# Pads of 32 bytes between tiles: the same matmuls, with operands that begin in other halves of a 64-byte line

## The chip, the core and the metric

The kernel runs on one core of one Trainium2 chip. The metric is the device time of one execution in microseconds; lower is better. A core has a matrix engine (TensorE, PE in the profile, with its weight loads shown apart as PEld), VectorE (DVE), ScalarE (ACT), GpSimd (POOL) and SyncE (SP), which issues most transfers. SBUF, the on-chip memory, has 128 partitions; a tile takes the same bytes of every partition, so one byte address says where it begins. In this text the *half* of a tile or operand is its first byte's address modulo 64, which is 0 or 32 for everything here.

## The reference: what is computed

One layer of an encoder, with the same weights, over 1024 and 256 tokens, 1024 wide; then a final RMSNorm. All in float32.

```python
n = _rms_norm(h, g_mix, NORM_EPS)
z = jnp.einsum('bsd,dc->bsc', n, w_in)                 # one input projection for both mixers
oa = _diff_attention(q, k, v, lam, slopes)             # 4 heads, two softmax maps each
ob = _gqa_attention(qb, kb, vb)                        # 8 query heads, 2 kv heads, rotary positions
h = h + jnp.einsum('bsc,cd->bsd', mixed, w_out)
n2 = _rms_norm(h, g_mlp, NORM_EPS)
a = jax.nn.relu(jnp.einsum('bsd,df->bsf', n2, w_ff1))  # 1024 -> 4096
h = h + jnp.einsum('bsf,fd->bsd', a * a, w_ff2)        # 4096 -> 1024
gate = jax.nn.sigmoid(jnp.einsum('bsd,de->bse', _rms_norm(h, g_ple, NORM_EPS), w_ple_gate))
h = h + gate * jnp.einsum('bsp,pd->bsd', p_l, w_ple_proj)
```

## The kernel before

**Products.** A float32 product is made of three matmuls of type float32r. Each operand is split into a high part (ScalarE copies it, rounded, into a float32r tile) and a low part (VectorE or GpSimd subtracts the high part from the original). The matmuls are high·high, high·low and low·high, accumulated in one PSUM bank. A matmul has a *stationary* operand of 128 columns, which a weight load brings into the array, and a *moving* operand of 128, 256, 384 or 512 columns, which streams through it. In the profile's names `out<-a,b` on PE, `a` is the moving operand and `b` the stationary one. The weight load of the next matmul runs while the present one streams, so what is read from SBUF at the same time is the moving operand of one matmul and the stationary operand of the next.

**Stages**, with their place in the profiled span. The order of the instructions on each engine is fixed in the program.

1. Input projections, to about 260 us: `psb` and `psv` take the weights as moving operand (256 columns) and the tokens `xh`, `xl` as stationary; `psa` the other way round, with 512 or 256 columns.
2. Attention with the output projection woven in, to about 750 us. `sc` are the scores, `tr` transposes of the probabilities, `av` the products with the values (`plan_unit.av`, line 720: moving `ph`, `pl`, 256 columns; stationary the value tile `vt128` or `vt256`). `pso` is the output projection (moving weights `ow`, 512 columns; stationary `mt`).
3. First MLP product, to about 1200 us, by Strassen's scheme: seven products for each of 16 column blocks of `w_ff1`. `Unit1.put` runs one product for two pieces of the tokens, 384 and 256 columns. Each piece is a run of 12 matmuls into one PSUM tile: eight with the moving operand `nhi` (the high part of the tokens, slots H0 to H6), then four with `nlo` (the low part, slots L1 to L7). Stationary is `w1` in a W slot. That is 7 × 16 = 112 runs of each length.
4. Second MLP product, to about 1547 us, again seven products, each over eight blocks (`NB`), so m = 0 to 55. `put2` runs 30 matmuls of 512 columns for each m: five tiles j of six matmuls. Moving is `wo`, stationary `ao`. The slots rotate with m % 3 (line 1339): `ao` in H0, H2, H3, and `wo` in H1, L7, L5.
5. Gate and embedding, to the end: ten token tiles; for each, eight transposes (`trg`), then twice 24 matmuls `psg` (moving the gate weights `gw`, stationary `n3`, 512 columns) followed by six matmuls `psp` (moving `pw`, stationary `p_h`, `p_l`). The last tile is cut into more pieces of 512 and 256 columns. `gate` has the elementwise work behind each `psg`, and lines 1601 to 1632 that of the embedding and the final norm.

**Where tiles begin.** Tiles come from pools that are stacked in SBUF from the left and from the right. A pool of `slot`s holds one buffer for each tag, and later tiles of other shapes take the same slot. `open_out_proj` opens the slots H0 to H6 and W0 to W8 on the right; L1 to L7, Q, K and W9 to W11 lie on the left. `TILES` lists the attention's buffers in the order in which they are laid down. The addresses below are read from the two built programs.

Of the kernel before, what the change touches and what calls it, by code (L numbers as in the profile page):

```python
# [14 lines left out]
F32 = mybir.dt.float32  # L15
F32R = mybir.dt.float32r
F16 = mybir.dt.float16
# [6 lines left out]
P = 128  # L24
D = 1024
KD = D // P
NP_TOK = 1024
NS_TOK = 256
T = NP_TOK + NS_TOK
NT = T // P  # L30
# [4 lines left out]
DISTW = 1920  # L35
# [5 lines left out]
def f(ap):  # L41
    return ap.bitcast(F32)
# [3 lines left out]
def encoder_kernel(ctx: ExitStack, tc: tile.TileContext, x, xT, pT, w_in, w_out, w_ff1, w_ff2, w_gate, w_proj,  # L46
# [11 lines left out]
    PHB = 4  # L58
# [37 lines left out]
    def pool(name, bufs=1, side=None, space=None, stack=None):  # L96
        kw = dict(name=name, bufs=bufs, reuse_waits="tile")
        if side:
            kw["side"] = side
        if space:  # L100
            kw["space"] = space
        return (stack or ctx).enter_context(tc.tile_pool(**kw))
# [32 lines left out]
    def rsqrt(dst, src, scale, eps, tp, n, tag):  # L135
        vv = tp.tile([P, n], F32, tag=f"{tag}v", name=f"{tag}v")
        uu = tp.tile([P, n], F32, tag=f"{tag}u", name=f"{tag}u")
        V.tensor_scalar(vv, src, scale, eps, op0=ALU.mult, op1=ALU.add)
        S.activation(uu, vv, AF.Ln)
        S.activation(dst, uu, AF.Exp, scale=-0.5)  # L140
        if n == 1:
            S.activation(uu, dst, AF.Copy, scale=-0.5)
            V.scalar_tensor_tensor(vv, dst, dst, vv, op0=ALU.mult, op1=ALU.mult)
            V.scalar_tensor_tensor(dst, vv, -3.0, uu, op0=ALU.add, op1=ALU.mult)
            return
        V.tensor_tensor(uu, dst, dst, op=ALU.mult)
        V.tensor_tensor(uu, uu, vv, op=ALU.mult)
        V.tensor_scalar(uu, uu, -0.5, 1.5, op0=ALU.mult, op1=ALU.add)
        V.tensor_tensor(dst, dst, uu, op=ALU.mult)
# [45 lines left out]

    def slot(tag, shape, dt, name):
        return slot_pool[tag].tile(shape, dt, tag=tag, name=name, bufs=1)

    def open_slots(pool_, tags):
        for tag in tags:  # L200
            slot_pool[tag] = pool_
            size = {"H": 2560, "L": 2560, "W": 1024, "Q": 1280, "K": 1280, "T": 512}[tag[0]]
            slot(tag, [P, size], F32, tag)
# [264 lines left out]
    def early_w1():  # L468
        for p in range(NEW):
            raws = [slot(f"Q{kh}", [P, 4, 256], F32, "w1e") for kh in range(2)]  # L470
            for kh, raw in enumerate(raws):
                load(raw, w_ff1[kh * 512:kh * 512 + 512, p * 256:(p + 1) * 256].rearrange("(k p) c -> p k c", p=P))
# [28 lines left out]
    def along(main, side, skip, every):  # L501
# [20 lines left out]
    TILES = {  # L522
        "o": ([P, 256], F32, 3), "or": ([P, 256], F32, 1), "ml": ([P, 2, 256], F32R, 1),
        "mm": ([P, 2], F32, 4), "ll": ([P, 2], F32, 4), "rl": ([P, 2], F32, 4), "osq": ([P, 256], F32, 1),
        "kt": ([P, T], F32R, 1), f"vt{P}": ([P, NT, P], F32R, 1), "ph": ([P, 2, 256], F32R, PHB),
        "pl": ([P, 2, 256], F32R, PLB), "qt": ([P, 2, 2, 256], F32R, QTB), "p": ([P, 1024], F32, PB),
        "dist": ([P, DISTW], F16, 1), f"vt{2 * P}": ([P, NT, 2 * P], F32R, 1), "pq": ([P, 256], F32, 4),
    }

    MT = 0  # L530
# [314 lines left out]
    def open_out_proj():  # L845
        xs.close()
        fr = pool("fr", side="right")
        open_slots(fr, [f"H{i}" for i in range(7)] + [f"W{i}" for i in range(9)])
        op_state["h"] = [slot(f"H{j}", [P, 2560], F32, "h_sb") for j in range(NT // 2)]

    TORD = (0, 1, 2, 3, 8, 9, 4, 5, 6, 7)
# [22 lines left out]
    def opw_split(raws):  # L874
        n = next(ow_n) % 5
        if n < 2:
            w = slot(f"H{5 + n}", [P, 2, D], F32R, "ow")
            a, b = w[:, 0], w[:, 1]
        else:
            a, b = (slot(f"W{2 * n - 4 + i}", [P, D], F32R, "ow")[:] for i in range(2))  # L880
        for i, raw in enumerate(raws):
            c = slice(i * 512, i * 512 + 512)
            S.activation(a[:, c], raw, AF.Copy)  # L883
            G.tensor_tensor(b[:, c], raw, f(a[:, c]), op=ALU.subtract)
        return a, b
# [504 lines left out]
    def load_h(half, n, tag):  # L1390
        t = hq[half, n] = slot(tag, [P, HP, 512], F32, "hq")
        dma(t, hd[half][:, :, n * 512:n * 512 + 512])
# [6 lines left out]
    def put2(m):  # L1399
        n, b = divmod(m, NB)  # L1400
        ah, al, bh, bl = OPS.pop(m)
        if b == 0:
            if O2[n] in (1, 7):
                acc[O2[n]] = slot({1: "H5", 7: "L4"}[O2[n]], [P, HP, 512], F32, "acc")
            banks_of[n] = [bank(tag, "f2_") for tag in BANKS[n].split()]
        for j in range(HP):
            c = slice(j * P, (j + 1) * P)
            pr = []
            for k in range(2):
                pr += [(ah[:, k, c], bh[:, k]), (ah[:, k, c], bl[:, k]), (al[:, k, c], bh[:, k])]  # L1410
            split3(banks_of[n][j], pr, b == 0, b == NB - 1)
            if b == NB - 1:
                evac2(O2[n], j, banks_of[n][j])
# [52 lines left out]
    gw, pw, n3 = [], [], {}  # L1466
    g_n = itertools.count()

    def w_raw(src):
        n = next(g_n)  # L1470
        t = slot("W10" if n < 4 else f"W{8 + n % 2}", [P, D], F32, "graw")
        dma(t, src)
        return t

    def gate_w(k, tags):
        raw = w_raw(w_gate[k * P:(k + 1) * P, :])
        if len(tags) == 1:
            t = slot(tags[0], [P, 2, D], F32R, "gw")
            a, b = t[:, 0], t[:, 1]
        else:  # L1480
            a, b = (slot(t, [P, D], F32R, "gw")[:] for t in tags)
        S.activation(a, raw, AF.Copy, scale=gple[:, k:k + 1])
        V.scalar_tensor_tensor(b, raw, gple[:, k:k + 1], f(a), op0=ALU.mult, op1=ALU.subtract)
        gw.append((a, b))

    def proj_w(k, tag):
        raw = w_raw(w_proj[k * P:(k + 1) * P, :])
        t = slot(tag, [P, 2, D], F32R, "pw")
        S.activation(t[:, 0], raw, AF.Copy)
        V.tensor_tensor(t[:, 1], raw, f(t[:, 0]), op=ALU.subtract)  # L1490
        pw.append((t[:, 0], t[:, 1]))

    gi_n = itertools.count()

    def h_half(t, n):
        j, half = divmod(TORD.index(t), 2)
        return h_of(j, half, n)

    def gate_input(t):

        n3_ = slot(("H5", "L4")[next(gi_n) % 2], [P, 2, KD, P], F32R, "n3")
        n3h, n3l = n3_[:, 0], n3_[:, 1]
        for n in range(2):
            tr = pp2[0].tile([P, 4, P], F32, tag="tr", name="trg", bufs=2)
            for k in range(4):
                PE.transpose(tr[:, k], h_half(t, n)[:, k * P:(k + 1) * P], ident)
            S.activation(n3h[:, 4 * n:4 * n + 4], tr, AF.Copy)
            V.tensor_tensor(n3l[:, 4 * n:4 * n + 4], tr, f(n3h[:, 4 * n:4 * n + 4]), op=ALU.subtract)
        ss = gq_.tile([P, 2], F32, tag="gss", name="gss")
        for n in range(2):  # L1510
            jk = gq_.tile([P, 512], F32, tag="gjk", name="gjk", bufs=1)
            S.activation(jk, h_half(t, n), AF.Square, accum_out=ss[:, n:n + 1])
        V.tensor_tensor(ss[:, 0:1], ss[:, 0:1], ss[:, 1:2], op=ALU.add)
        rn = gq_.tile([P, 1], F32, tag="grn", name="grn")
        rsqrt(rn, ss[:, 0:1], 1.0 / D, 1e-6, gq_, 1, "grs")
        S.activation(rn, rn, AF.Copy, scale=-1.0)
        return n3h, n3l, rn

    QUADS = {2: (0, 0, "H6"), 3: (0, 1, "L2"), 4: (1, 0, "H4"), 5: (1, 1, "L3")}
    for m in range(NM):  # L1520
        put2(m)
        if m in QUADS:
            load_h(*QUADS[m])
        if m + 3 < NM:
            prep(m + 3)

        if m >= 4 * NB and m % 4 == 0 and len(gw) < 4:
            gate_w(len(gw), KTS[2 * len(gw):2 * len(gw) + 2])
        if m == NM - 4:
            fqs.close()  # L1530
            gq_ = pool("gq", side="left", bufs=2)
            for k in range(2):
                gate_w(4 + k, (ARS[k],))
        elif m == NM - 3:
            gate_w(6, (AOS[m % 3],))
            gate_w(7, (WOS[m % 3],))
            n3[FORD[0]] = gate_input(FORD[0])
        elif m == NM - 2:
            proj_w(0, AOS[m % 3])
            proj_w(1, WOS[m % 3])  # L1540
            n3[FORD[1]] = gate_input(FORD[1])
# [4 lines left out]
    for ti, t in enumerate(FORD):  # L1546
# [70 lines left out]
        i = 2 if last else 1  # L1617
        V.tensor_tensor(ss[:, 0:1], ss[:, 0:1], ss[:, i:i + 1], op=ALU.add)
        if last:

            for (n0, nn), e in zip(pieces[1:], es[1:]):
                V.tensor_tensor(e, h_half(t, 1)[:, n0 - 512:n0 - 512 + nn], gfin[:, n0:n0 + nn], op=ALU.mult)
        rf = gq_.tile([P, 1], F32, tag="rf", name="rf")
        rsqrt(rf, ss[:, 0:1], 1.0 / D, 1e-6, gq_, 1, "rf")
        if last:
            for (n0, nn), e in zip(pieces[1:], es[1:]):
# [2 lines left out]
        for n0 in range(0, 512 if last else D, 512):  # L1629
            n = slice(n0, n0 + 512)  # L1630
# [54 lines left out]
```

## Time and profile before

| | |
|---|---|
| device time, median of 3 runs | 1704.38 us (1703.62 to 1708.34) |
| span of the profiled execution, first to last instruction | 1703.2 us |
| PE busy | 1666.5 us, 98% |
| PEld, DVE, ACT, POOL busy | 87%, 69%, 51%, 39% |
| granted TensorE clock, mean | 0.997 |

No time other than the span is given for the profiled execution itself; the median of the runs is 1.2 us above it. A matmul's duration in the profile reaches past the start of the next one, since matmuls are pipelined: a lone one of the 512-column kind shows some 393 ns, while they start every 227 to 235 ns. So the number that counts is the *pace*, the time from one start to the next. It is read from two views: the chain of waits, whose pieces give the time that a run of matmuls took and their number, and the timeline, whose rows give the start of each run.

### The profile page before, as it was taken

Reading aid. Unit: us, or ns where it says so; the run is one execution under the profiler, and the core shown is the slowest. Engines: PE = TensorE matmul, PEld = TensorE weight load, DVE = VectorE, ACT = ScalarE, POOL = GpSimd, SP = SyncE. Lnnn points to the kernel's source line nnn. Section 1 sums busy time; section 2 is a strip of 40 time slices with the busy share of each in tenths; the row PEclk is TensorE's granted clock in tenths of the full one; section 3 lists DMA queues with packets and bytes.
Section 4 is the critical chain, followed back from the end, with each engine's and each line's share of the span. In section 5 each row is a group of like instructions: output and inputs, shape, how many; then the busy total and the mean of one; then the engine's idle time right before and its main releaser. Section 6 shows DMA issues by size and latency. Waiting matters only on the chain.

```text
span 1703.2 us, 27269 instructions
## 1 busy us (share of the span) xinstructions
PE 1666.5 (98%) x9849; PEld 1488.6 (87%) x9849; DVE 1177.2 (69%) x2119; ACT 868.3 (51%) x1749; POOL 658.4 (39%) x647
## 2 busy tenths in 40 slices
PE   8999999999899999999999999999999999999997
PEld 8999889888788888889999999998888888888886
DVE  7788588787887878578666666665655865445666
ACT  8543377677766767674333233333433333354644
POOL 1224455555653445424655666520533400001441
PEclk9999999999999999999999999999999999999999
DMA  9767844433953624495343434359666466532111
GB/s 316 228 225 246 233 141 124 138 92 108 269 156 118 165 69 127 134 308 181 132 156 127 138 131 150 122 198 376 202 216 195 130 205 193 169 114 73 35 44 50
DMA packets 191867, 278.28 MB, mean 163 GB/s; under 512 B 13674, under 2 KB 121076, under 8 KB 191732
## 3 DMA queue, kind: packets, MB, share of 16 engines
q1 hardware_dynamic: 189988, 271.28, 49.7%
q0 software_dynamic: 1600, 5.24, 1.0%
q8 instruction: 78, 1.28, 0.3%
q14 instruction: 57, 0.47, 0.1%
q10 hardware_dynamic: 144, 0.00, 0.0%
HBM read 182.63 MB, written 88.61 MB: 159 GB/s over the span
## 4 chain that ended last, share of the span: by engine, by line
PE 79%; DVE 7%; ACT 4%; issue 4%; DMA 3%; POOL 3%; SPq 0%; POOLq 0%; ACTq 0%; DVEq 0%
PE psa L255 6%; PE sc L642 5%; PE psb L255 5%; PE av L720 5%; PE pso L255 4%; PE tr L696 3%; PE psv L255 3%; PE psg L1576 2%; DVE pl L707 1%; DMA h_sb<-in_x 1%; DVE mm L659 1%; PE f__16295 L156 1%; PE f__15255 L156 1%; PE f__16637 L156 1%; PE f__15600 L156 1%
## 5 line engine op out<-in xcount | busy, mean ns | idle before, releaser
L1373 ACT ACTIVATE ao<-ar 128x1280 fp32r<-128x1280 f32 x56 | 71.3, 1275 | 187.5 <-PE f__16299 L156 37.8
L642 PE MATMUL sc<-kt,qt 128*128 128x512 f32 (+1 forms) x576 | 157.0, 392 | 6.9 <-ACT p L667 4.6
L707 DVE TENSOR_TENSOR pl<-tr,ph 128x512 fp32r<-128x512 f32 x204 | 137.9, 684 | 33.5 <-ACT ph L702 32.3
L1375 DVE TENSOR_TENSOR ao<-ar,ao 128x1280 fp32r<-128x1280 f32 x56 | 93.3, 1666 | 94.0 <-ACT ao L1373 94.0
L702 ACT ACTIVATE ph<-tr 128x512 fp32r<-128x512 f32 x204 | 119.8, 595 | 56.9 <-PE tr L696 50.4
L255 PE MATMUL pso<-ow,mt 128*128 128x512 f32 x480 | 119.4, 395 | 4.2 <-ACT ow L883 1.8
L696 PE MATMUL tr<-ident,p 128*128 128x128 f32 x768 | 116.0, 274 | 5.7 <-DVE pl L707 4.9
L642 PEld LDWEIGHTS sc<-kt,qt 128*128 128x128 f32 x576 | 99.4, 190 | 24.8 <-ACT p L667 6.1
L1576 PE MATMUL psg<-gw,n 128*128 128x512 f32 (+1 forms) x504 | 115.4, 384 | 0.0
L696 PEld LDWEIGHTS tr<-ident,p 128*128 128x128 f32 x768 | 91.8, 141 | 22.5 <-DVE pl L707 8.6
L1576 PEld LDWEIGHTS psg<-gw,n 128*128 128x128 f32 x504 | 90.8, 188 | 19.5
L255 PEld LDWEIGHTS pso<-ow,mt 128*128 128x128 f32 x480 | 87.5, 188 | 22.4 <-DVE osq L747 2.0
L1094 POOL TENSOR_SCALAR w1r<-w1r,gmlp 128x256 f32<-128x256 f32 x112 | 79.7, 728 | 67.6 <-DMA w1r<-in_w_ff 67.6
L720 PE MATMUL av<-ph,vt 128*128 128x256 f32 x544 | 102.4, 289 | 1.1 <-ACT ph L702 0.5
L681 POOL TENSOR_SCALAR p<-p,rl 128x1024 f32<-128x1024 f32 x64 | 76.0, 1188 | 51.3 <-DVE rl L679 46.6
L1167 ACT ACTIVATE w<-w1s 128x512 fp32r<-128x512 f32 x56 | 35.2, 628 | 116.5 <-POOL w1s L1174 49.4
L659 DVE TENSOR_REDUCE mm<-sc 128x1 f32<-128x1024 f32 (+1 forms) x80 | 84.2, 1055 | 8.8 <-PE sc L642 8.3
L720 PE MATMUL av<-pl,vt 128*128 128x256 f32 x408 | 89.5, 301 | 0.0
L720 PEld LDWEIGHTS av<-ph,vt 128*128 128x128 f32 x544 | 82.4, 190 | 6.6 <-ACT ph L702 0.9
L667 ACT ACTIVATE p<-sc,mm 128x1024 f32<-128x1024 f32 x64 | 71.3, 1114 | 25.5 <-DVE mm L659 18.5
L655 DVE CUSTOM_DVE_ANT_0 p<-sc,dist 128x1024 f32<-128x1024 f32 x64 | 77.6, 1218 | 7.9 <-PE sc L642 3.8
L664 ACT ACTIVATE p<-p,mm 128x1024 f32<-128x1024 f32 x64 | 73.5, 1149 | 18.0 <-DVE mm L655 17.3
(1520 smaller groups left out, 4717.2 us busy)
## 6 DMA issues: line engine op xcount, KB each, us to landing
ar<-ad SPq DMA_DIRECT2D x56, 640.0 KB, 4.0
w2r<-in_w_ff SPq DMA_DIRECT2D x56, 512.0 KB, 4.6
qt<-qd SPq DMA_DIRECT2D x160, 128.0 KB, 3.1
ad<-q SPq DMA_DIRECT2D x64, 320.0 KB, 3.0
ad<-qs SPq DMA_DIRECT2D x48, 320.0 KB, 2.2
w1r<-in_w_ff SPq DMA_DIRECT2D x28, 512.0 KB, 4.3
md<-ml SPq DMA_DIRECT2D x40, 256.0 KB, 2.5
mt<-md SPq DMA_DIRECT2D x20, 512.0 KB, 5.4
```

Source lines behind the costliest of these rows:

```text
L255: PE.matmul(ps, a, b, start=i == 0, stop=i == n - 1)
L642: PE.matmul(ps[:, h0:h0 + n], shared["q"][:, cc, v, i * P:(i + 1) * P], kt[:, s0 + h0:s0 + h0 + n], start=v == 0, stop=v == 1)
L655: V.tensor_tensor_reduce(out=p[:, :sn], in0=ps[:, :sn], in1=dst_t[:, off:off + sn], scale=SLOPES[idx], scalar=3.0e38, op0=ALU.add, op1=ALU ...
L659: V.tensor_reduce(out=st["m", i][:, 0:1], in_=ps[:, :sn], axis=AX.X, op=ALU.max, negate=True)
L681: G.tensor_scalar(p[:, :sn], p[:, :sn], rl[:, 0:1], 1.0, op0=ALU.mult, op1=ALU.mult)
L696: PE.transpose(t[:, jj, i * P:(i + 1) * P], st["ws"][i][:, j * P:(j + 1) * P], ident)
L702: S.activation(ph, st["tr", j2], AF.Copy)
L707: V.tensor_tensor(pl, st["tr", j2], f(st["ph", j2][:]), op=ALU.subtract)
L720: PE.matmul(st["av"][:, :256], x_, y_, start=j2 == 0 and n == 0, stop=j2 == nj - 1 and n == len(pr) - 1)
L1094: G.tensor_scalar(raw[:, k], raw[:, k], gmlp[:, 4 * kh + k:4 * kh + k + 1], 1.0, op0=ALU.mult, op1=ALU.mult)
L1375: V.tensor_tensor(ao[:, 1], a, f(ao[:, 0]), op=ALU.subtract)
L1576: ends[:] = [PE.matmul(ps, a, b, start=m == 0, stop=m == len(pr) - 1)]
```

## The change

The instructions, their order on every engine, their waits and their semaphore updates are the same in both built programs. What differs is where tiles begin, in four ways.

- Small unused tiles of 8 float32 (32 bytes for each partition) are laid down between others: `pad0` to `pad3` ahead of and behind the two value tiles in `TILES`, one between the H and the W slots, and `gpad` at the start of the last stage's pool `gq`.
- `slot32` makes a tile 8 elements longer than asked for and returns the view from the eighth element on, so that it begins 32 bytes into its slot. `at32` is the same function. The output projection's weights in H5 and H6, the single-slot gate weights, the embedding weights `pw` and the normed tokens `n3` use them.
- Ahead of that, the slots H0 to H6 have moved down by 32 bytes through the pad between H and W.
- The tile `rf` has one buffer where it had two, which makes room for `gpad`.

| matmul, columns | count | half of the moving operand: before, after | half of the stationary operand: before, after |
|---|---|---|---|
| `av<-ph,vt` and `av<-pl,vt`, 256 | 952 | 0, 0 | 0, **32** |
| `pso<-ow,mt`, 512 | 480 | 32, 32 | 32, 32 |
| first MLP product, `nhi,w1`, 384 and 256 | 872 of each | 32, **0** | 32, 32 |
| first MLP product, `nlo,w1`, 384 and 256 | 436 of each | 0, 0 | 32, 32 |
| first MLP product with `w1` in W9 to W11 (3 runs of each length): `nhi` | 24 of each | 32, **0** | 0, 0 |
| second MLP product, `wo` in L7 or L5, 512 | 1110 | 0, 0 | 32, **0** |
| second MLP product, `wo` in H1, 512 | 570 | 32, **0** | 32, **0** |
| `psg<-gw,n`, 512 and 256 | 504 | 0 in 189, 32 in 315; after **32** in all | 0 in 264, 32 in 240; after **32** in all |
| `psp<-pw,p`, 512 and 256 | 126 | 32, 32 | 0, **32** |

All other matmuls keep their halves (`psb`, `psv`, `psa`, `sc`), or are transposes whose stationary input moves (`h_sb`, `hq`). Before, every matmul operand with half 0 begins below byte 110,000 of its partition and every one with half 32 above byte 120,000. After, `ao`, `nhi` and the `wo` in H1 begin above 120,000 with half 0, and `vt`, `p_h` and `p_l` below 110,000 with half 32.

```diff
+    def slot32(tag, shape, dt, name):
+        n = int(np.prod(shape[1:]))
+        t = slot(tag, [P, n + 8], dt, name)[:, 8:]
+        dims = " ".join("abc"[:len(shape) - 1])
+        return t.rearrange(f"p ({dims}) -> p {dims}", **dict(zip("abc", shape[1:]))) if len(shape) > 2 else t
+
+    def at32(tag, *args):
+        return slot32(tag, *args)
...
-        "kt": ([P, T], F32R, 1), f"vt{P}": ([P, NT, P], F32R, 1), "ph": ([P, 2, 256], F32R, PHB),
+        "kt": ([P, T], F32R, 1), "pad0": ([P, 8], F32, 1), f"vt{P}": ([P, NT, P], F32R, 1), "pad1": ([P, 8], F32, 1), "ph": ([P, 2, 256], F32R, PHB),
...
-        "dist": ([P, DISTW], F16, 1), f"vt{2 * P}": ([P, NT, 2 * P], F32R, 1), "pq": ([P, 256], F32, 4),
+        "dist": ([P, DISTW], F16, 1), "pad2": ([P, 8], F32, 1), f"vt{2 * P}": ([P, NT, 2 * P], F32R, 1), "pad3": ([P, 8], F32, 1), "pq": ([P, 256], F32, 4),
...
-        open_slots(fr, [f"H{i}" for i in range(7)] + [f"W{i}" for i in range(9)])
+        open_slots(fr, [f"H{i}" for i in range(7)])
+        fr.tile([P, 8], F32, name="pad")
+        open_slots(fr, [f"W{i}" for i in range(9)])
...
-            w = slot(f"H{5 + n}", [P, 2, D], F32R, "ow")
+            w = slot32(f"H{5 + n}", [P, 2, D], F32R, "ow")
...
-            t = slot(tags[0], [P, 2, D], F32R, "gw")
+            t = at32(tags[0], [P, 2, D], F32R, "gw")
...
-        t = slot(tag, [P, 2, D], F32R, "pw")
+        t = at32(tag, [P, 2, D], F32R, "pw")
...
-        n3_ = slot(("H5", "L4")[next(gi_n) % 2], [P, 2, KD, P], F32R, "n3")
+        n3_ = at32(("H5", "L4")[next(gi_n) % 2], [P, 2, KD, P], F32R, "n3")
...
             gq_ = pool("gq", side="left", bufs=2)
+            gq_.tile([P, 8], F32, name="gpad", bufs=1)
...
-        rf = gq_.tile([P, 1], F32, tag="rf", name="rf")
+        rf = gq_.tile([P, 1], F32, tag="rf", name="rf", bufs=1)
```

## The prediction, made before the changed kernel was run

> **What bounds the kernel now.** I read the page's first part and the span first, then the busy time by stretches, then the chain of waits and the timeline inside each stage. The page and the stretches:
>
> ```profile
> span 1703.2 us, 27269 instructions
> PE 1666.5 (98%) x9849; PEld 1488.6 (87%) x9849; DVE 1177.2 (69%) x2119; ACT 868.3 (51%) x1749; POOL 658.4 (39%) x647
> ```
> ```profile
> core 0: us, PE busy (x) PEld busy (x) DVE busy (x) ACT busy (x) POOL busy (x), PEclk, DMA share, GB/s
> 400.00:740.00 340.00, 325.09 (x1963) 280.21 (x1963) 263.91 (x508) 235.51 (x496) 167.29 (x184) 0.99 0.53 155
> 790.00:1190.00 400.00, 400.00 (x2633) 393.82 (x2633) 258.53 (x419) 138.95 (x264) 195.02 (x185) 1.00 0.49 171
> 1240.00:1540.00 300.00, 300.00 (x1303) 243.64 (x1302) 168.79 (x152) 113.53 (x131) 45.23 (x21) 1.00 0.54 173
> 1540.00:1703.20 163.20, 153.74 (x731) 126.72 (x729) 102.53 (x188) 82.02 (x216) 48.79 (x40) 0.98 0.13 45
> ```
>
> In the two MLP stages (790 to 1540 us) PE never stops, at full granted clock, and the busiest other engine, VectorE, has 258.53 of 400 us and 168.79 of 300. There a nanosecond of pace is a nanosecond of the end. In the attention (400 to 740) PE stands 15 of 340 us. So the question is what sets the pace of matmuls that wait for nothing. The chain of waits in the second MLP product shows matmuls of one shape at two paces (pieces of one tile j, six matmuls of 512 columns; columns: start, length, what):
>
> ```profile
> 1302.85 1.39 PE f__15255 L156 x6
> 1305.60 1.36 PE f__15257 L156 x6
> 1308.32 1.36 PE f__15259 L156 x6
> 1309.68 1.40 PE f__15255 L156 x6
> 1322.28 1.40 PE f__15259 L156 x6
> ```
>
> 1.36 / 6 = 226.7 ns, 1.40 / 6 = 233.3 ns. By the slots, the five tiles from 1302.85 have `wo` in H1 (moving half 32, stationary 32: the *same* half), those from 1309.68 on have it in L7, then L5 (0 and 32: *different* halves). The gate stage has all four pairs in one line of code, at 512 columns:
>
> ```profile
> 1549.14 3.40 PE psg L1576 x15
> ```
> ```profile
> 1552.54 1.40 PE psg L1576 x6
> ```
> ```profile
> 1562.92 2.10 PE psg L1576 x9
> ```
> ```profile
> 1565.02 1.39 PE psg L1576 x6
> ```
> ```profile
> 1555.79 1.38 PE psg L1576 x6
> ```
>
> In order: 32 and 32 run 226.7; moving 0 with stationary 32 run 233.3; moving 32 with stationary 0 run 233.3; 0 and 0 run 231.7 in the first six matmuls after a different pair. The last row is 32 and 32, again the first six behind something else: 230. So a same pair needs about six matmuls to settle, and up to there 0 with 0 looks like 32 with 32. That is the reading on which the forecast rests: at 512 columns the *relation* of the two halves sets the pace, 226.7 same and 233.3 different.
>
> With shorter moving operands the relation works the other way round. The first MLP product, chain first (runs of 12), then the timeline (starts; a length there reaches past the next start):
>
> ```profile
> 907.35 1.43 PE f__11906 L156 x12
> 908.78 2.11 PE f__11949 L156 x12
> ```
> ```profile
> 905.08 1.58 PE L156 MATMUL f__11893<-nhi,w 128*128 128x384 f32 x8
> 906.49 0.86 PE L156 MATMUL f__11893<-nlo,w 128*128 128x384 f32 x4
> 907.19 1.12 PE L156 MATMUL f__11906<-nhi,w 128*128 128x256 f32 x8
> 908.15 0.64 PE L156 MATMUL f__11906<-nlo,w 128*128 128x256 f32 x4
> 908.62 0.69 PE L156 MATMUL f__11949<-nhi,w 128*128 128x384 f32 x3
> ```
> ```profile
> 757.99 1.55 PE L156 MATMUL f__10408<-nhi,w 128*128 128x384 f32 x8
> 759.38 0.87 PE L156 MATMUL f__10408<-nlo,w 128*128 128x384 f32 x4
> ```
> ```profile
> 776.91 1.10 PE L156 MATMUL f__10504<-nhi,w 128*128 128x256 f32 x8
> 777.84 0.40 PE L156 MATMUL f__10524<-nlo,w 128*128 128x256 f32 x2
> ```
> ```profile
> 25.18 5.60 PE psv L255 x48
> ```
>
> `nhi` with `w1` in a right-hand slot is a same pair (32, 32): (906.49 − 905.08) / 8 = 176 ns at 384 columns and 0.96 / 8 = 120 at 256. `nlo` is a different pair (0, 32): 0.70 / 4 = 175 and 0.47 / 4 = 117.5. The two rows at 757.99 and 776.91 are the few runs with `w1` on the left, where `nhi` is a different pair: 1.39 / 8 = 173.8 and 0.93 / 8 = 116.3. And `psv`, a different pair (0, 32) in a long run of 256 columns: 5.60 / 48 = 116.7.
>
> **The change part by part.** No instruction and no wait is added, so each part is a count of matmuls by a difference of paces.
>
> *Second MLP product.* 56 blocks m of 5 × 6 matmuls; `wo` lies in L7 or L5 in 37 of them, in H1 in 19. All become 0 and 0. 37 × 5 × (1.40 − 1.36) = 7.4 us. The first piece behind a change of relation (1.39 instead of 1.36) falls away in the 19 others: 19 × 0.03 = 0.6. I take 7.8, the rows being rounded; bounds 8.0, and +0.4 (a loss) if 0 with 0 stayed at the 1.39 that its first six show: 185 × (1.39 − 1.40) + 95 × (1.39 − 1.36) − 0.6.
>
> *First MLP product.* 109 of 112 runs of each length become different pairs throughout. With 173.8 and 116.7 a run takes 2.09 and 1.40: (0.02 + 0.03) × 109 = 5.5, and with 116.3 for all 256-column ones 5.9. With the paces of `nlo`, 175 and 117.5, it is 2.10 and 1.41: 3.3. I take 5.0, nearer to the first, since those rows are eight in a row as the changed ones are. The three runs with `w1` on the left become same pairs and lose under 0.2 us.
>
> *Gate and embedding.* One tile's matmuls, with `n3` on the left:
>
> ```profile
> 1562.23 5.58 PE psg L1576 x24
> 1567.80 1.40 PE psp L156 x6
> 1569.20 5.58 PE psg L1576 x24
> 1574.78 1.40 PE psp L156 x6
> 1577.06 5.57 PE psg L1576 x24
> 1582.65 0.70 ACT ge L1580
> ```
> ```profile
>   ACT ge L1580: 34.1, 18
> ```
>
> That is 13.96 us for 60 matmuls; all same they take 60 × 0.2267 = 13.60 and some 0.04 to settle, 0.32 less. The next tile, with `n3` at 32, begins with 5.57, so it has nearly as much to gain. Nine tiles: 2.9, the upper bound. Against it: from 1582.65 on the chain of waits runs over ScalarE and VectorE, which follow PE closely here. The last row (who waited for `psg`) says that ScalarE still stood waiting for PE, 34.1 us in 18 times, 1.9 on average, before the exponential of each gate half; PE needs to gain 0.16 a half, so most of that cover stays. If it did not, only the two tiles before 1582 gain: 0.6. I take 2.2.
>
> *Attention.* The 952 `av` matmuls go from same (0, 0) to different (0, 32):
>
> ```profile
> 553.73 2.63 PE av L720 x22
> ```
> ```profile
> PE tr L696 <- DVE pl L707: 5.1, 9, 1.1
> PE sc L642 <- ACT p L667: 4.6, 6, 1.7
> ```
>
> 119.5 ns now against 116.7 for a different pair: at most 952 × 2.8 = 2.7 us. They come in fours and sixes between transposes and scores, too short to settle, and PE waits in this stage for VectorE and ScalarE, which get no faster. Between 0 and 2.7 I take 1.0.
>
> *The other engines* write to moved tiles. VectorE's `n3` subtraction, which alternates between half 0 and half 32, shows no difference (smallest, median and largest duration in ns):
>
> ```profile
> L1508 DVE TENSOR_TENSOR n<-trg,n x20: 679/691/692, 1535.3 to 1670.3; 128x512 fp32r<-128x512 f32 x20
> ```
>
> I cost them at nothing. `rf` with one buffer brings no wait, since the two programs' waits are equal.
>
> *Sum.* 7.8 + 5.0 + 2.2 + 1.0 = 16.0 us. On the profiled span that is 1703.2 − 16.0 = 1687.2, and on the median of the runs, 1.2 above the span, 1704.4 − 16.0 = 1688.4. All bounds low: 8.0 + 5.9 + 2.9 + 2.7 = 19.5, so 1684.9. With the second product at 7.4 and the others at 3.3, 0.6 and 0: 11.3, so 1693.1.
>
> **The rivals.**
>
> *It is not the half but the place.* Before the change each half goes with one end of SBUF: 0 below byte 110,000, 32 above 120,000. Every row above would read the same if matmuls met the weight load differently when both operands lie at one end. Pads of 32 bytes then do nothing: 1704.4. For it: no row separates the two. Against it: the sign turns between 512 and 384 columns within differences of 3 to 7 ns, which looks like two streams that fall in or out of step, and a shift of 8 elements is 3 to 4 ns at 226.7 ns for 512.
>
> [...]
>
> *0 with 0 does not settle at 512 columns.* The second product gives its +0.4 and the rest stays: 1704.4 + 0.4 − 5.0 − 2.2 − 1.0 = 1696.6. For it: no row shows 0 with 0 beyond the first matmuls. Against it: row for row these equal 32 with 32.
>
> *The moving operand's half alone decides at 512 (32 fast), and the place in the run, not the half, decides in the shorter ones.* Then H1's blocks fall from 1.36 to 1.40: 19 × (5 × 0.04 − 0.03) = +3.2; the 171 gate matmuls whose moving half goes from 0 to 32 win 171 × 6.6 ns = 1.1; the first product and `av` stay. 1706.5, slower. It decides if the 0 with 0 row keeps 1.39 or more in steady state. Against it: the row 1562.92 has moving 32 and runs 233.3.
>
> **How the numbers follow.** Forecast 0.78 (own range 1685 to 1693), place instead of half 0.11, 0 with 0 unsettled 0.08, moving half alone 0.03. The likeliest time is 1688.4. The forecast and the unsettled case hold 0.86 together, so the range reaches from a little under the lowest bound, 1683, to 1697. About 0.3%, 5 us, is what a measurement can tell from no change. Faster by more: nearly all of the forecast and of the unsettled case, 0.83. Within: the place, and what these two miss, 0.14. Slower: 0.03.
>
> **What would show it.** In the second product every piece of six at 1.36, none at 1.40; if they read 1.39, 0 with 0 does not settle. In the first product runs of 12 at 2.08 to 2.10 and 1.40 to 1.41, still with no idle PE. In the gate 24 matmuls in 5.45 to 5.50, and ScalarE's wait before L1580 smaller but there. Pieces at 1.36 and 1.40 alternating as before would show that the place decides. I am wrong, too, if the paces come as forecast and the end does not: then VectorE or ScalarE bounds the last stage.

## The result, and the profile after

The changed kernel takes 1690.83 us (median of 4 runs, 1689.4 to 1692.11) against 1704.76 before: a ratio of 0.9915, with a 95% interval of 0.9902 to 0.9927. A second set of five runs gave 1692.16, ratio 0.9921 (0.9908 to 0.9935). The forecast was 1688.4 with a range of 1683 to 1697. The profiled execution took 13.1 us less than before, the forecast's sum is 16.0. What follows is mostly about those 3 us, and about what the word "half" in the forecast stands for.

The page of the changed kernel, its first part:

```profile
span 1690.1 us, 27269 instructions
PE 1651.6 (98%) x9849; PEld 1482.7 (88%) x9849; DVE 1179.9 (70%) x2119; ACT 868.0 (51%) x1749; POOL 661.0 (39%) x647
```

The busy time by stretches, with the columns as in the prediction (the two MLP stages, then the last stage):

```profile
785.00:1185.00 400.00, 400.00 (x2666) 394.32 (x2665) 261.51 (x424) 139.45 (x265) 199.84 (x191) 1.00 0.50 174
1235.00:1533.00 298.00, 298.00 (x1324) 246.63 (x1323) 173.30 (x155) 114.84 (x134) 44.26 (x21) 1.00 0.54 175
1533.00:1690.10 157.10, 146.08 (x704) 122.34 (x702) 97.95 (x185) 79.28 (x212) 48.77 (x40) 0.98 0.12 43
```

PE still never stops in the MLP stages, at the same granted clock, but 2666 matmuls begin in 400 us where 2633 did. The changed kernel's line numbers are higher by 9 in the attention and by 12 in the gate: L1588 is `psg` (L1576 before), L1592 the exponential `ge` behind it (L1580 before).

The second MLP product, in the chain of waits (start, length, what):

```profile
1290.99 1.36 PE f__15262 L156 x6
...
1296.43 1.36 PE f__15261 L156 x6
...
1310.04 1.36 PE f__15261 L156 x6
```

Of 222 whole pieces of six that the chain shows between 1228 and 1534 us, 219 read 1.36, whichever slot `wo` has; none alternates with 1.40. The first product, in the chain and then in PE's timeline:

```profile
898.35 1.42 PE f__11837 L156 x12
899.76 2.09 PE f__11862 L156 x12
```
```profile
898.19 1.11 PE L156 MATMUL f__11837<-nhi,w 128*128 128x256 f32 x8
899.13 0.63 PE L156 MATMUL f__11837<-nlo,w 128*128 128x256 f32 x4
899.60 1.56 PE L156 MATMUL f__11862<-nhi,w 128*128 128x384 f32 x8
901.00 0.86 PE L156 MATMUL f__11862<-nlo,w 128*128 128x384 f32 x4
901.69 1.11 PE L156 MATMUL f__11875<-nhi,w 128*128 128x256 f32 x8
```

At 384 columns `nhi` takes 1.40 / 8 = 175 and `nlo` 0.69 / 4 = 172.5 ns. At 256 columns it is 0.94 / 8 = 117.5 and 0.47 / 4 = 117.5, in a run of 1.42 us where 1.40 to 1.41 was forecast. The gate, in the chain, and who waited for `psg`:

```profile
1549.62 5.50 PE psg L1588 x24
1555.13 1.36 PE psp L156 x6
1556.49 5.44 PE psg L1588 x24
1561.93 1.38 PE psp L156 x6
...
1563.34 0.93 POOL hq L1615
```
```profile
  ACT ge L1592: 25.2, 14
```

24 matmuls take 5.50 and 5.44 us where they took 5.58, so PE does what was forecast. ScalarE's wait for it went from 34.1 us in 18 times to 25.2 in 14. The attention, where 22 `av` matmuls took 2.63:

```profile
553.65 2.60 PE av L729 x22
```

Where the time went, by the starts in both timelines (a pace is the mean of the start-to-start times that hold no wait; the change in us is over all starts of the group):

| part | pace before, after (ns) | change, us | forecast |
|---|---|---|---|
| second MLP product, 512 columns | 231.4, 226.7 | −7.6 | −7.8 |
| first product: `nhi` 384; `nhi` 256 | 177.2, 174.4; 119.5, 118.4 | −3.5 | |
| first product: `nlo` 384; `nlo` 256 | 174.3, 173.4; 118.7, 118.0 | −0.8 | −5.0 with the row above |
| gate and embedding, `psg` at 512 | 231.7, 227.6 | −2.3 with `psp` | −2.2 |
| attention: `ph`; `pl` | 119.1, 118.0; 118.8, 117.2 | −1.5 with its waits (−1.25 by the paces alone) | −1.0 |
| all other starts, waits among them | | +1.1 | 0 |
| from the last matmul's start to the end | | **+1.5** (9.74, now 11.27) | 0 |

With 0.1 less ahead of the first matmul that makes the 13.1. `nlo` and `w1` keep their halves, and still `nlo` became faster by 0.7 to 0.9 ns; it runs right behind `nhi`, which moved, and it is back at its old paces when `nhi` alone goes back (w1_undone, below). So the pace of a pair is not fixed by its two starts alone. The waits of the attention vary from run to run: over the profiles of the kernels whose value tiles lie as in the change, the `av` groups, waits included, differ from before by −2.5 to +0.2 us.

The row of +1.5 us is the one that the forecast did not have. ScalarE's exponentials of the last tiles in its timeline, and PE's last groups, of the kernel before:

```profile
1678.32 0.69 ACT L1580 ACTIVATE ge<-psg,grn 128x512 f32<-128x512 f32 x1 [0.96 <-PE psg L1576]
1686.80 0.67 ACT L1580 ACTIVATE ge<-psg,grn 128x512 f32<-128x512 f32 x1
```
```profile
1679.52 11.42 PE L1576 MATMUL psg<-gw,n 128*128 128x512 f32 x72
```

and of the changed kernel:

```profile
1664.12 0.67 ACT L1592 ACTIVATE ge<-psg,grn 128x512 f32<-128x512 f32 x1
1673.64 0.67 ACT L1592 ACTIVATE ge<-psg,grn 128x512 f32<-128x512 f32 x1
```
```profile
1658.11 5.60 PE L1588 MATMUL psg<-gw,n 128*128 128x512 f32 x24
1664.91 11.36 PE L1588 MATMUL psg<-gw,n 128*128 128x512 f32 x72
```

Before, ScalarE waited 0.96 us for PE at 1678.32, and then took the last tile's first piece 7.28 us after its matmuls began. Now it waits for PE neither time (no bracket), and takes that piece 8.73 us after its matmuls began, 1.45 us later. The matmuls have moved ahead of the elementwise work of the tile before, and the time that they gained waits there.

### The profile page after: what moved, and what is told of

Same layout as the page of the kernel before. It is cut to its first block, busy times and chain, and to the rows that moved or that the text cites. A ratio compares the mean times of both kernels' runs of the same rounds, so it can differ in the third digit from the quotient of the medians.

```text
span 1690.1 us, 27269 instructions
## 1 busy us (share of the span) xinstructions
PE 1651.6 (98%) x9849; PEld 1482.7 (88%) x9849; DVE 1179.9 (70%) x2119; ACT 868.0 (51%) x1749; POOL 661.0 (39%) x647
## 4 chain that ended last, share of the span: by engine, by line
PE 79%; DVE 8%; ACT 4%; issue 4%; POOL 2%; DMA 2%; POOLq 0%; SPq 0%; ACTq 0%; DVEq 0%
PE psa L264 6%; PE sc L651 6%; PE av L729 5%; PE psb L264 4%; PE pso L264 4%; PE tr L705 4%; PE psv L264 2%; PE psg L1588 1%; DVE pl L716 1%; DVE p L686 1%; DMA xt<-in_x 1%; POOL hq L1615 1%; DMA xr<-in_xT 1%; PE f__15605 L156 1%; PE f__16642 L156 1%
## 5 line engine op out<-in xcount | busy, mean ns | idle before, releaser
L1588 PE MATMUL psg<-gw,n 128*128 128x512 f32 (+1 forms) x504 | 113.7, 381 | 0.0
L1588 PEld LDWEIGHTS psg<-gw,n 128*128 128x128 f32 x504 | 90.9, 188 | 17.8
```

The source lines that it names most:

```text
L1588: ends[:] = [PE.matmul(ps, a, b, start=m == 0, stop=m == len(pr) - 1)]
```

## The experiments

All were run with the changed kernel as their base unless it is said otherwise. They fall into three groups: is it the relation of the two starts, and part by part; what is the relation's period; and what takes the 1.5 us at the end. `slot_at(off, ...)` is `slot32` with `off` elements of 4 bytes in the place of 8.

### The second product alone made different: w2_diff

```diff
-        wo = slot(WOS[m % 3], [P, 2, 2, 512], F32R, "wo")
+        wo = slot_at(8, WOS[m % 3], [P, 2, 2, 512], F32R, "wo")
```

> The changed kernel, with the moving operand wo of the second MLP product 32 bytes into its slots (32) against ao at 0, so that all 1680 matmuls of that stage are different pairs. Theory (the relation of the two halves sets the pace, 226.7 ns same and 233.3 ns different at 512 columns): every piece of six takes 1.40 us, the stage 1680 x 6.6 ns = 11.1 us more, about 1702 us. Rival (the moving operand's own half decides, 32 is fast): pieces stay at 1.36 us, about 1691 us.

Measured: 1701.78 us, ratio to the kernel before 0.9983 (0.9974 to 0.9992). Pieces in the chain:

```profile
1325.13 1.40 PE f__15609 L156 x6
1326.54 1.40 PE f__15605 L156 x6
```

All of the second product has the slow pace, 233.3 ns on average, also the blocks that were at 1.36 in the kernel before. 1701.8 − 1690.8 is 11.0 us (9.6 from the change's second set); 1680 × (233.3 − 226.7) ns is 11.1. The moving operand now has the half 32 throughout, so the rival that a moving half of 32 is fast by itself at 512 columns falls. That it is a matter of the place in SBUF falls too: `wo` and `ao` lie in the slots where they lay.

### The first product alone put back: w1_undone

```diff
         open_slots(fr, [f"H{i}" for i in range(7)])
-        fr.tile([P, 8], F32, name="pad")
         open_slots(fr, [f"W{i}" for i in range(9)])
...
-            w = slot32(f"H{5 + n}", [P, 2, D], F32R, "ow")
+            w = slot(f"H{5 + n}", [P, 2, D], F32R, "ow")
...
     def at32(tag, *args):
-        return slot32(tag, *args)
+        return (slot if tag[0] == "H" else slot32)(tag, *args)
...
-        wo = slot(WOS[m % 3], [P, 2, 2, 512], F32R, "wo")
+        wo = slot_at(0 if WOS[m % 3][0] == "H" else 8, WOS[m % 3], [P, 2, 2, 512], F32R, "wo")
```

Without the pad the H slots begin 32 bytes higher; the tiles in them that began 32 bytes into their slot begin at its start now, which is the same address. The second product has 32 with 32, and the first has what it had before the change.

> The changed kernel without the pad between the H and W slots, so that nhi is at 32 again as w1 is (same pairs, as before the change); wo in L5 and L7 is put at 32 so that the second product keeps same pairs (32 and 32), and gate, embedding and attention keep their halves. Theory: the first product's runs of 12 go back to 2.11 and 1.43 us, which is worth the 4 to 5 us that they gained; 1695 to 1696 us; the second product stays at 1.36 for six, with wo in the low end of SBUF and ao in the high one. Rival (the place in SBUF sets the pace and 32 bytes do nothing): no stage moves, 1691 us, or the second product shows 1.40 wherever wo and ao lie at different ends.

Measured: 1694.98 us, ratio 0.9946 (0.9929 to 0.9962), 4.2 us more than the change (2.8 more than its second set). The first product's runs of 12 in the chain:

```profile
898.36 1.43 PE f__11836 L156 x12
899.79 2.11 PE f__11861 L156 x12
```

These are the lengths before the change, and the four mean paces are back to 177.1, 174.3, 119.5 and 118.7. The second product stays at 226.8 with both operands at 32, in 37 of its 56 blocks (`wo` in L7 or L5) with one operand at each end of SBUF. So the first product's part is 4.2 us by the clock and 4.3 by the timelines (4.2 between the timelines of w1_undone and the change).

### The gate alone made different: gate_diff

```diff
-        n3_ = at32(("H5", "L4")[next(gi_n) % 2], [P, 2, KD, P], F32R, "n3")
+        n3_ = slot_at(0, ("H5", "L4")[next(gi_n) % 2], [P, 2, KD, P], F32R, "n3")
```

> The changed kernel, with n3 at 0 and all gate weights at 32, so that the 456 gate matmuls of 512 columns are different pairs. Both theories: PE needs 456 x 5.8 ns = 2.6 us more in this stage (24 matmuls in 5.60 us instead of about 5.46). If PE sets the end, the end comes 2.6 us later, 1693.4 us, and the time from the last matmul to the end stays 11.3 us. If the elementwise work behind the gate sets the end, the end comes less than 1.5 us later and the time from the last matmul to the end shrinks from 11.3 to about 9.7 us, what it was before the change.

Measured: 1693.09 us, ratio 0.9929 (0.9914 to 0.9944). That is 2.3 us above the change's first set and 0.9 above its second, and the interval overlaps that of the change, so the clock does not tell the two theories apart. In the chain and in ScalarE's timeline of the last tiles:

```profile
1550.14 5.59 PE psg L1593 x24
...
1557.10 5.59 PE psg L1593 x24
```
```profile
1666.19 0.69 ACT L1597 ACTIVATE ge<-psg,grn 128x512 f32<-128x512 f32 x1 [1.02 <-PE psg L1593]
1674.60 0.67 ACT L1597 ACTIVATE ge<-psg,grn 128x512 f32<-128x512 f32 x1
```

The gate's pace is 232.9, and PE's `psg` matmuls of 512 columns take 2.3 us more than in the change. But the time from the last matmul's start to the end is 9.73 again, not 11.3 as it would be if PE set the end, and ScalarE waits for PE again at 1666.19. In the profiles, then, the end wins back 1.5 of the 2.3 us that PE lost. The spans agree (1691.0 against 1690.1, 0.9 more), but single executions of the change differ by more than that.

### Steps of 16 bytes: by16 and by48

```diff
-        wo = slot(WOS[m % 3], [P, 2, 2, 512], F32R, "wo")
+        wo = slot_at(4, WOS[m % 3], [P, 2, 2, 512], F32R, "wo")
...
-        n3_ = at32(("H5", "L4")[next(gi_n) % 2], [P, 2, KD, P], F32R, "n3")
+        n3_ = slot_at(4, ("H5", "L4")[next(gi_n) % 2], [P, 2, KD, P], F32R, "n3")
```

In by16 the tokens `xh`, `xl` of the projections also begin 16 bytes into their buffers, which are 32 bytes longer, and the value tiles begin at 16 instead of 32. In by48 the 4 of the two lines is a 12 (48 bytes), the tokens begin 48 bytes into buffers that are 64 longer, and the value tiles begin at 48.

> The changed kernel with four operands moved by 16 bytes: wo at 16 against ao at 0; n3 at 16 against gate weights at 32; xh and xl at 48, against wh, wl at 0 (psv, psb) or 32 (psa); vt at 16 against ph at 0. If only the 32-byte half counts in which an operand begins: second product as same pairs, 1.36 us for six; gate as different pairs, 1.40 for six; psv (0 and 48) 5.60 us for 48 as now. If only equal starts count as same: second product 1.40, gate 1.40. If the distance counts in finer steps: other paces than these two, and perhaps lower ones.

> The changed kernel, with the weights wo 48 bytes into their slots (ao at 0), n3 at 48 (gate weights at 32), the tokens xh and xl of the projections at 16 where they have 0, and the value tiles at 48. It mirrors the run with steps of 16: there wo at 16 with ao at 0 ran 231.7 ns, not settled, and n3 at 16 with the gate weights at 32 ran 227.3. Theory A (the distance from the stationary start to the moving one decides, also in steps of 16): the distance is minus 16 in both stages now, plus 16 before, so both stages read alike, whatever the pace. Theory B (a moving operand that begins off a step of 32 pays by itself, a stationary one doesn't): as in the run with 16, second product about 231.7, gate about 227.3, span about 1697. Theory C (only the 32-byte half that holds the start counts): second product 233.3 (48 is in the upper half), gate 226.7, span 1701.

Measured: 1698.89 us in by16 and 1700.86 in by48, a single run each. Pieces of the second product and of the gate in by16, then in by48:

```profile
1326.38 1.39 PE f__15604 L156 x6
```
```profile
1563.63 5.44 PE psg L1593 x24
1571.30 5.47 PE psg L1593 x24
```
```profile
1336.65 1.38 PE f__15604 L156 x6
...
1340.81 1.40 PE f__15602 L156 x6
```
```profile
1565.54 5.44 PE psg L1593 x24
1573.21 5.59 PE psg L1593 x24
```

With 16 the second product runs 231.7 ns on average and the gate 227.3; with 48 they run 231.7 and 229.3. So 16 bytes are seen: `wo` at 16 lies in the same 32-byte half as `ao` at 0 and is not at 226.7. The reading by halves falls, for starts that these pads do not use. The reading by distance alone (theory A of by48) falls by by16 as well: there the moving start lies 16 bytes above the stationary one in both stages, and the paces differ. In by48 the two distances, 48 and −16, are the same only modulo 64. Theory B had the second product right and the gate wrong by 2 ns; theory C, whose 1701 is near the time, had both paces wrong. The projections, whose tokens moved too, hardly answer: `psv` (256 columns) runs 117.3 and 118.2 ns where the change has 117.2.

In by48 the first group of a tile (behind the transposes) runs 233 and the second (behind `psp`) 227, at starts that are the same modulo 512. The two read different columns of the gate weights, but that is not it: in the first token tile, where the groups begin behind the embedding's matmuls, 27 gate matmuls in a row take 6.12 us (the chain of by48 at 1545.67) and 18 more 4.08, so 45 of that tile's 48 run at 226.7 ns. So in by48 the pace also went by what ran just before: 233 behind the transposes, 227 behind `psp`.

### Steps of 64 and 128 bytes: by64 and by128

```diff
-        wo = slot(WOS[m % 3], [P, 2, 2, 512], F32R, "wo")
+        wo = slot_at(16, WOS[m % 3], [P, 2, 2, 512], F32R, "wo")
...
-        n3_ = at32(("H5", "L4")[next(gi_n) % 2], [P, 2, KD, P], F32R, "n3")
+        n3_ = slot_at(24, ("H5", "L4")[next(gi_n) % 2], [P, 2, KD, P], F32R, "n3")
```

In by128 the two numbers are 32 and 40.

> The changed kernel, with the weights wo of the second MLP product 64 bytes into their slots (ao stays at the slots' start, 0 modulo 64) and the normed tokens n3 of the gate 96 bytes into theirs, where the change has 32 (the gate weights stay at 32). Modulo 64 both pairs are what they are in the changed kernel. Theory (the relation of the two starts modulo 64): pieces of six at 1.36 us in the second product, 227 ns in the gate, span 1690 us. Rival (the starts repeat only after 128 bytes, so that 64 apart is a different pair): 1.40 and 233 ns, span 1690 + 11 + 1 = 1702 us.

> The changed kernel, with wo 128 bytes into its slots (ao at the slots' start) and n3 160 bytes into theirs (gate weights at 32): the starts of both pairs are the same modulo 64 and modulo 128, and 128 apart modulo 256. The run with 64 bytes gave 228.9 ns in the second product and 233.3 in the gate, so the pattern doesn't repeat after 64. Theory (it repeats after 128): 226.7 and 227 ns, pieces of six at 1.36 us, span 1690 us. Rival (it repeats after 256 or more): another pace in at least one of the two stages, span 1692 to 1702 us.

Measured: 1695.44 us and 1704.27, a single run each. In all four single runs `nhi`, whose starts did not move, keeps the paces that it has in the change (174.3 to 174.4 ns and 118.3 to 118.4). Pieces of the second product and of the gate in by64, then in by128:

```profile
1330.18 1.37 PE f__15605 L156 x6
```
```profile
1559.82 5.60 PE psg L1593 x24
```
```profile
1325.28 1.40 PE f__15608 L156 x6
```
```profile
1561.54 5.58 PE psg L1593 x24
```

64 apart gives 228.9 in the second product and 233.3 in the gate; 128 apart gives 233.3 and 232.7. The theory missed in both: "modulo 64" is wrong, and so is modulo 128. The rival of by64 had the gate right and the second product wrong, and by128 came 2.3 us above its rival's range. In the programs before and after the change every operand of the two MLP stages and of the gate, moving or stationary, begins at 192 or at 224 modulo 256. There "the same half" and "the same start modulo 256" are one and the same, which is why the prediction's rows could not tell them apart. That 256 apart counts as equal is seen in the embedding alone: `pw` begins at 480 modulo 512 and `p_h`, `p_l` at 224, and the piece of six at 1555.13, quoted above, takes 1.36 us; it took 1.40 with `p_h`, `p_l` at 192. It is a group of six, not a long run. The paces at 512 columns, by the two starts modulo 512:

| stage | fixed start | the other operand's start: pace in ns |
|---|---|---|
| second product, stationary | 448 | moving at 448: 226.7; 464: 231.7; 480: 233.3; 496: 231.7; 0: 228.9; 64: 233.3 |
| gate, moving | 480 | stationary at 480: 227.6; 464: 227.3; 448: 232.9; 496: 229.3; 32: 233.3; 96: 232.7 |

Equal starts are the fastest of the six in one stage and within 0.3 ns of the fastest in the other.

### The elementwise work behind the gate: late3, late10, before_late10

In the gate stage the product `d * e` and the subtraction from `h` are GpSimd's, except in the last two token tiles, where they are VectorE's. The experiments give VectorE more tiles (late3 the last three, late10 all ten):

```diff
-        late = ti >= NT - 2
+        late = ti >= NT - 10
```

> The changed kernel, with VectorE in place of GpSimd for two elementwise steps behind the gate (the product d * e and the subtraction from h) in the last three token tiles, not in the last two alone. Paces of the matmuls stay. In the changed kernel the time from the last matmul's start to the end grew from 9.74 to 11.27 us, since the elementwise loop (about 15 us a token tile) is slower than PE (14.54). Theory (the chain of that loop sets the end): two GpSimd steps of 1.29 and 1.41 us twice a tile become VectorE steps of about 0.69, so the chain comes up to 1.3 us earlier in one tile: tail 10 to 10.5 us, 0.5 to 1.3 us faster than the change, 1689.5 to 1690.3. Rival (the end is set by the last tile's own chain, which begins with its matmuls): no change, 1690.8, or slower by up to 1 us, since VectorE gets 2.8 us more work in that tile.

> As the run before, in all ten token tiles of the gate stage. Theory (the loop falls behind PE tile by tile and ends late): with the loop under PE's 14.54 us a tile nothing is carried into the last tile, the tail is back at 9.7 us or under, 1.5 us faster than the change: 1689.3. Rival (VectorE, 9.9 us busy of 15 and 2.8 us more then, becomes the one that is late): no gain or a loss of up to 3 us, 1690.8 to 1694.

Measured: 1689.72 us with three tiles (ratio 0.9912, 0.9895 to 0.9929) and 1689.28 with ten (0.9907, 0.9892 to 0.9922), as expected. The time from the last matmul's start to the end is 9.73 and 9.81 us, against 11.27 in the change, with the same paces on PE. Both intervals overlap that of the change, so the change and late10 were run once more side by side, and the same edit was made in the kernel before:

> The changed kernel itself once more, beside the next run on the same chip, since their difference (1690.8 against 1689.3 in different sets of runs) lies within both intervals. All theories: 1690.3 to 1691.5, time from the last matmul's start to the end 11.3 us.

> The kernel with VectorE for the two elementwise steps in all ten token tiles, once more. Theory (the elementwise loop behind the gate sets the end of the changed kernel, by 1.5 us): 1.0 to 2.0 us under the run before, tail 9.7 to 9.8 us. Rival (the earlier difference was between sets of runs): within 0.5 us of the run before.

> The kernel before, with VectorE for the same two elementwise steps in all ten token tiles. Theory (at the old pace PE needs 14.8 us a tile and the loop keeps up, so that the last tile's matmuls set the end): no gain, 1704.3 to 1705.3, tail 9.7 us as before. Rival (the loop sets the end before the change as well): 1 us or more faster, under 1703.8.

Measured: the change 1692.16 (0.9921, 0.9908 to 0.9935), with ten tiles on VectorE 1690.04 (0.9914, 0.9900 to 0.9928), the kernel before with the same edit 1705.83 (1.0009, 0.9999 to 1.0019). The first is 0.7 us and the last 0.5 us above the upper end of what was expected. The times at the end are 11.17, 9.82 and 9.82 us. The chain of waits of late10_again over the last two tiles, and ScalarE in the last tile:

```profile
1657.03 5.44 PE psg L1593 x24
1662.47 1.36 PE psp L156 x6
1663.83 11.19 PE psg L1593 x72
1675.02 1.40 PE psp L156 x6
```
```profile
1669.31 0.69 ACT L1597 ACTIVATE ge<-psg,grn 128x512 f32<-128x512 f32 x1 [0.59 <-PE psg L1593]
```

The chain stays on PE to 1676 us, and ScalarE waits for PE again in the last tile. So the edit wins 2.1 us in medians on top of the pads (1.5 between the earlier sets, which were not run side by side) and nothing without them. In the traces it is plain (1.46 and 1.35 us at the end, in the two pairs of profiles); by the clock the direction is the same both times, but the intervals overlap, and the size is not settled. late10 has the lowest median of the kernels tried here, 1689.28 (1690.04 when it was run again); late3, at 1689.72, cannot be told apart from it.

The time at the end against the gate's pace, over the kernels with GpSimd in eight tiles, shows the same exchange:

| kernel | pace of `psg`, ns | last matmul's start to the end, us |
|---|---|---|
| by64 | 233.3 | 9.14 |
| gate_diff | 232.9 | 9.73 |
| by128 | 232.7 | 9.66 |
| before | 231.7 | 9.74 |
| by48 | 229.3 | 10.51 |
| the change | 227.6 | 11.27, 11.17 |
| w2_diff | 227.5 | 11.17 |
| by16 | 227.3 | 11.55 |
| w1_undone | 227.2 | 11.31 |

## Why the prediction was right, and where it was off

**What bounds the kernel.** Right: in the MLP stages each nanosecond of pace came out at the end. The second product gave 7.6 of 7.8 us in the timeline, and making all of it slow in w2_diff cost 11.0 of 11.1.

**"The relation of the two halves sets the pace."** Right, for the starts in the two kernels, as to which pair is faster. It is shown by undoing one stage alone, by the clock for the two MLP products (w2_diff, w1_undone) and by the pace for the gate (gate_diff); the attention was not undone by itself. That the relation alone sets the pace is too strong: `nlo` changed its pace at unchanged starts, and the gate of by48 shows two paces at equal ones. As a statement about halves of a 64-byte line it is wrong: starts 64 or 128 bytes apart have equal halves and run at 228.9 to 233.3 ns (by64, by128). What the rows supported was: equal starts modulo 256 against starts 32 apart. The sum held because the pads only move starts between these two.

**0 with 0 settles at 512 columns.** Right: 226.7 in 1680 matmuls. The rival that it does not, with 1696.6, falls.

**First product, 5.0 us.** It gave 4.3 (4.2 by w1_undone). The term that was mis-sized is the 256 columns: I took the 116.3 of eight matmuls in a row and `psv`'s 116.7 as the settled pace. Within the changed runs the pace does not settle; consecutive starts vary from 116 to 122 ns, and the mean is 118.4 for `nhi`. By the paces the 256 columns gave 1.3 us where 0.03 × 109 = 3.3 had been taken. At 384 columns it does settle, at 173.4 within a run (173.8 was taken), and they gave 2.8 where 0.02 × 109 = 2.2 had been taken. The bounds of 3.3 and 5.9 hold it.

**Gate and embedding, 2.2 us.** PE gained 2.3, but 1.5 of it was lost again by the end, so about 0.8 is left. The failed step is "PE needs to gain 0.16 a half, so most of that cover stays". The 1.9 us of wait were a mean over 18 times. In the kernel before, the wait at the tile before the last was 0.96 and the last tile had none; the gain of the tiles adds up, and in the last tile the finished matmuls wait until the elementwise work of the tiles before is done. The chain of waits on ScalarE and VectorE from 1582 us on, which I had quoted, said so. The low bound of 0.6, taken for that case, is near what came. The warning sign that I had named (paces as forecast, end not) is what happened here, for this one term.

**Attention, 1.0 us.** 1.25 by the paces, 1.5 with the waits of this run. The size of the waits varies by more than that between runs, so nothing finer can be said.

**No cost on the other engines and no wait from `rf`.** Nothing in the profiles speaks against it. It was not tried by itself.

The sum with the two sizes corrected is 7.6 + 4.3 + 0.8 + 1.5 = 14.2 us; the remaining 1.1 of the profiled difference are waits elsewhere, of the size by which these vary between runs. In late10_again, where the end follows PE, the span is 15.8 us under the kernel before; the medians are 14.5 under it there and 16.0 in late10.

## What to carry to other kernels

When PE never stops, read the pace (start to start) and group it by the starts of the moving operand and of the next matmul's stationary operand, modulo as much as the tiles' own strides allow: here equal starts were the fast choice at 512 columns (226.7 ns against 233.3), 32 bytes apart at 384 (174.4 against 177.2) and 256 (118.4 against 119.5). Before giving the rule a period, ask which starts occur at all; two values cannot show one. And a mean wait of an engine (here 1.9 us, with none in the last tile) is no cover for a gain that adds up over tiles: look at the last tile's wait, and whether the loop behind PE keeps PE's new period.

## What of the hardware was unexpected

Start addresses move the pace by up to 3% with nothing else changed: 226.7 to 233.3 ns at 512 columns. At 384 and 256 the differences are smaller and the other way round: `nhi` has a mean of 177.2 and 119.5 with equal starts, 174.4 and 118.4 with starts 32 apart. The sign turns between 512 and 384 columns; why was not found. Steps of 16 bytes count: with `wo` 16 bytes from `ao` the second product runs 231.7 ns, with equal starts 226.7. At 512 columns the pattern repeats neither after 64 bytes (228.9 and 233.3 ns in the two stages of by64) nor after 128 (233.3 and 232.7 in by128). That it repeats after 256 is seen only in the embedding's groups of six (1.36 us, and 1.40 with starts 32 apart modulo 256). At the same starts modulo 512 the pace can be either of two (227 or 233 in by48), by what ran before.

The weight load of the next matmul and the running matmul overlap in time: in the second product, in the profiles before and after, a load begins 3 ns after the start of the matmul before its own and is done 191 ns after it (medians), while the matmuls start 231.4 and 226.7 ns apart. The two are not independent of each other: in w2_diff, 32 bytes between the starts of their operands cost 11.0 us. The profiles do not show when each operand is read, so whether it is the reads that collide is not shown.
